# Attention with its join one head behind: statistics, scalings and loads in another order

## The chip, the cores and the metric

The kernel runs on one core of one Trainium2 chip. The metric is the device time of one execution in microseconds; lower is better. The core has a matrix engine (PE), a vector engine (DVE), a scalar engine (ACT), GpSimd (POOL) and SyncE (SP), whose queue issues nearly all DMAs of this kernel. Each engine runs its own instructions in a fixed order and waits on semaphores for the others.

## The reference

A decoder trunk of two layers on 1024 tokens of width 1024, in float32. Layer 0 mixes tokens by dilated attention in three groups (window 128 at dilation 1, 512 at 4, 2048 at 16) with 8 heads of 128; layer 1 by gated linear attention. Each is followed by an MLP of width 4096 with a squared ReLU. The change is in layer 0's attention, so the rest is left out here:

```python
def dilated_group_attention(q, k, v, dil, n_back):
    ...
    s = jnp.where(mask, s, -jnp.inf)
    m = jnp.max(s, axis=-1, keepdims=True)
    p = jnp.exp(s - m)
    l = jnp.sum(p, axis=-1)
    o = jnp.einsum('bzhnqk,bzhnkd->bzhnqd', p, vb) / l[..., None]
    lse = m[..., 0] + jnp.log(l)
    ...

def dilated_attention(h, w_in, w_out):
    B, S, _ = h.shape
    qkv = (h @ w_in).reshape(B, S, N_GROUPS, 3, ATTN_HEADS, HEAD_DIM)
    cos, sin = rope_tables(S, HEAD_DIM)
    outs, lses = [], []
    for g, (window, dil) in enumerate(DILATED_GROUPS):
        q = apply_rope(qkv[:, :, g, 0], cos, sin) * (HEAD_DIM ** -0.5)
        k = apply_rope(qkv[:, :, g, 1], cos, sin)
        v = qkv[:, :, g, 2].astype(jnp.float32)
        o_g, lse_g = dilated_group_attention(q, k, v, dil, window // dil)
        outs.append(o_g)
        lses.append(lse_g)
    alpha = jax.nn.softmax(jnp.stack(lses, axis=0), axis=0)
    o = jnp.sum(alpha[..., None] * jnp.stack(outs, axis=0), axis=0)
    return o.reshape(B, S, ATTN_WIDTH).astype(h.dtype) @ w_out
```

So the three groups' outputs of a head are added with weights that depend on the maximum `m` and the sum `l` of all three groups' rows. The kernel scales the exponentials `p` by these weights (the "scaled probabilities") and then multiplies by the values.

## The kernel before, in words

**Planes and slots.** Layer 0's q and k columns are computed in 24 planes, `p = 3h + g` for head `h` and group `g`. A plane is a product of the normed tokens with 256 columns by a seven-product scheme, each product in two halves of six matmuls: 14 slots, at the end of each of which `advance()` runs what an agenda holds for that slot. `at(slot, fn, rank)` puts a function there; functions of one slot run by rank. This order of calls is the order of the instructions on every engine, so a slot number or a rank in the code moves instructions between neighbours of the same engine, and nothing else does.

**Weights of the next plane.** `load(p + 1)` (L1436) issues four DMAs on SP that bring the raw weights, `stage` splits and combines them on ACT (L791) and DVE (L792, L819, L820, L828, L829).

**Columns and ropes.** Products accumulate in PSUM. `keep` copies a bank to `e` on ACT (L1484), `column` adds a bank and an `e` on DVE (L1444) to `c`, two DMAs (L1445, L1446) write `c` with its halves swapped to `cw`, and some slots later the rope (`turn` in `column`: L1453, L1454 and L1456, or L1461 for groups 1 and 2) makes a half of `qT` or `kT` from both on DVE.

**Scores.** One plane behind, `follow(p - 1)` computes the scores of group `g` (PE L1203, or L1292 for group 2, the "classes"), reduces them on DVE (L1225, L1301), takes the exponential on ACT (L1227, L1303), and `send` writes the statistics `st` (maxima and sums) to DRAM (L1234, L1308).

**The join of a head.** When head `h - 1` has its three groups, `Join(h - 1)` runs across the second plane of head `h`, in the steps that `join_steps` lists by slot:

- `begin` loads all statistics (L1344, L1345, L1348); `factors` makes the weights of the groups on DVE and ACT (L1358 to L1364, ACT at L1360).
- `spread` multiplies the exponentials by the factors: groups 0 and 1 block by block on ACT (L1239), group 2 in one DVE instruction (L1311).
- `load_values` loads `v` of each group (L1178 group 0, L1181 group 1, L1186 group 2).
- `turn_classes` transposes group 2's scaled exponentials on PE (L1318), `copy_classes` copies them to `pt` on ACT (L1388), `values_classes` multiplies by `v` (PE L1326), `keep_classes` copies the result to `oc` (ACT L1394).
- Groups 0 and 1 follow in halves: `turn` (PE L1262), `copy` (ACT L1400), `values` (PE L1271); `join` adds `oc` (DVE L1411).

PE runs all this between the matmuls of the plane (L854). The tables `HEAD` and `LAST` hold the slots of these steps, counted from the slot of `factors`. The last head's join runs in `tail`, among the output projection's matmuls (L196 to L198), with the loads of earlier heads' outputs (`turned.load`, L1798, and `early`, L1842) and of rows of x (`load_x`, L1780) on the same SP queue.

Of the kernel before, what the change touches and what calls it, by code (L numbers as in the profile page):

```python
# [27 lines left out]
NG = 3  # L28
# [13 lines left out]
def hybrid_trunk(ctx, tc, x, norm_mix, norm_mlp, norm_fin, a_in, a_out, g_in, g_up, g_b, g_nw,  # L42
# [219 lines left out]
    class Split:  # L262
# [4 lines left out]
        @staticmethod  # L267
        def at(tiles, k):
            n = 4 // len(tiles)
            return tiles[k // n][:, k % n, :]  # L270
# [1008 lines left out]
            at(c + send, self.send)  # L1279

    class Classes(Attention):
        SOFT = 9, 9, 9, 10
        SEND = 11

        def scores(self, j):
# [132 lines left out]
    class Heads(Up):  # L1418
# [20 lines left out]
        def column(self, p, b, half, bank_, e):  # L1439

            h, g = divmod(p, NG)
            c = t2([P, 512], F32, "c")
            w = t2([P, 512], F32, "cw")
            dve.tensor_tensor(c, bank_, e, op=OP.add)  # L1444
            sp.dma_start(w[0:64, :], c[64:128, :])  # L1445
            sp.dma_start(w[64:128, :], c[0:64, :])  # L1446

            def turn():
                sl = slice(512 * half, 512 * half + 512)
                if (p, b) not in self.dst:  # L1450
                    self.dst[p, b] = k4([P, S], F32, ("qT", "kT")[b])
                dst = self.dst[p, b]
                dve.tensor_tensor(w, w, ctab[:, 1, sl], op=OP.mult)  # L1453
                dve.tensor_tensor(c, c, ctab[:, 0, sl], op=OP.mult)  # L1454
                if g == 0:
                    dve.tensor_tensor(dst[:, sl], c, w, op=OP.add)  # L1456
                else:
                    r = 4 if g == 1 else 16
                    n = 512 // r
                    o = dst.rearrange("p (r m) -> p r m", r=r)[:, :, n * half:n * half + n]  # L1460
                    dve.tensor_tensor(o, c.rearrange("p (m r) -> p r m", r=r),  # L1461
                                       w.rearrange("p (m r) -> p r m", r=r), op=OP.add)
            wait = 3 if p == self.count - 1 and half else 4
            if g == 0 and half:
                wait = (5, 8)[b]
            at(clock[0] + wait, turn, 6)

        def remain(self, fn):
# [7 lines left out]
        def plan(self, p):  # L1476
            c = 14 * p
            st = self.st.setdefault(p, {})
            self.behind = True

            def keep(b, name):
                def fn():
                    e = t2([P, 512], F32, name)
                    act.activation(e, st[b], AF.Copy)  # L1484
                    st[name] = e
                return fn
            at(c + 3, keep("X", "e1"), 0)
            at(c + 5, lambda: self.column(p, 0, 0, st["Y"], st["e1"]), 1)
            at(c + 7, keep("V", "e5"), 0)
            at(c + 9, keep("X", "e2"), 0)  # L1490
            at(c + 11, lambda: self.column(p, 1, 0, st["V"], st["e2"]), 1)
            at(c + 13, keep("X", "e3"), 0)
            at(c + 13, lambda: self.column(p, 1, 1, st["X"], st["e5"]), 1)
            at(c + 15, lambda: self.column(p, 0, 1, st["Z"], st["e3"]), 1)
            if p == 0:
                for s, t in ((4, 1), (6, 3), (5, 5)):
                    at(c + t, lambda s=s: self.stage(p, s), 7)
            at(c + 3, lambda: self.load(p + 1), 5)
            for s, t in ((0, 8), (1, 9), (2, 10), (3, 11), (4, 14), (6, 15), (5, 17)):
                at(c + t, lambda s=s: self.stage(p + 1, s), 1.5 if s in (1, 3, 6) else 7)  # L1500

# [11 lines left out]
        def follow(self, p, c, points=None, soft=None, send=None):  # L1513
            h, g = divmod(p, NG)
            a = groups[h, g] = (Classes if g == 2 else Attention)(g, h, None, None)
            points = points or self.POINTS

            def begin():
                a.qT, a.kT = self.dst.pop((p, 0)), self.dst.pop((p, 1))
            at(c + points[0], begin, 0)  # L1520
            a.plan(c, points, soft or a.SOFT, send or a.SEND)

# [25 lines left out]
        keep_head(h, half, o)  # L1548
        reached.add((0, half))

    HEAD = dict(s2=2, v2=-1, v1=1, sp0=(0, 1, 1, 2), t2=4, o2=5)
    LAST = dict(s2=1, v2=1, v1=4, sp0=(1, 1, 3, 3), t2=5, o2=6)

    def join_steps(load, first, w, gap=1):

        n = lambda k: first + int(gap * k)
        t = 5
        pairs = ((0, 2), (4, 6), (1, 3), (5, 7))
        steps = [(load, 5, "begin"), (n(0), 9, "factors"), (n(w['s2']), 9.1, "spread", 2, None)]
        steps += [(n(w['v2']), 4, "load_values", 2), (n(1), 5, "load_values", 0), (n(w['v1']), 5, "load_values", 1)]  # L1560
        steps += [(n(w['sp0'][i]), 9, "spread", 0, range(2 * i, 2 * i + 2)) for i in range(4)]
        steps += [(n((5, 5, 7, 7)[i]), 9, "spread", 1, pairs[i]) for i in range(4)]
        steps += [(n(w['t2']), 3, "turn_classes"), (n(w['o2']), 0.6, "copy_classes"),
                  (n(w['o2']), 4, "values_classes"), (n(7), 0.5, "keep_classes")]
        order = ((0, 0), (1, 0), (0, 1), (1, 1))
        for i, (g, half) in enumerate(order):
            steps += [(n(t + i), 3, "turn", g, half), (n(t + i + 1), 0.6, "copy", g, half),
                      (n(t + i + 1), 0.65, "values", g, half)]
        return steps + [(n(t + 3), 0.5, "join", 0), (n(t + 5), 0.6, "join", 1)]
# [200 lines left out]
    class Turned:  # L1770
# [6 lines left out]
        def load_x(self, tb):  # L1777
            if tb < NB and tb not in self.loaded:
                self.loaded.add(tb)
                sp.dma_start(self.xs[tb // 2][:, tb % 2, :], self.src_x[128 * tb:128 * tb + 128, :])  # L1780
# [27 lines left out]
    for p in range(heads.count):  # L1808
        h, g = divmod(p, NG)
        if g == 0 and h:  # L1810
            Join(h - 1, joined).plan(14 * p, join_steps(15, 21, HEAD))
        if p == heads.count - 1:
            for k in range(0, KT, 2):
                add_rows(a_out, k)
            c = 14 * p
            at(c + 1, lambda: turned.load(0), 0)
            at(c + 3, lambda: (W.dma(), W.dma()), 0)
            at(c + 4, lambda: (W.dma(), W.dma()), 0)
            for t in (7,8,9,10):
                at(c + t, lambda: W.prep(dve), 7)  # L1820
            at(c + 8, lambda: turned.turn(0), 7)
            at(c + 9, lambda: (turned.load_x(0), turned.load_x(1)))
            at(c + 11, lambda: turned.turn(1), 7)
        heads.run_head(p)
# [7 lines left out]
    def tail():  # L1832

        c = clock[0]
        heads.follow(heads.count - 1, c, (7, 7, 8, 8), (9, 9, 10, 10), 11)
        turned.load(1)
        Join(HEADS - 1, last_joined).plan(c, join_steps(15, 19, LAST, 1.5))
        rows = {}

        def early(half):  # L1840
            t = rows[half] = h8([P, 4, 512], F32, "ol2")
            sp.dma_start(t[:, 0:3, :], oscr[4:7, :, 512 * half:512 * half + 512].rearrange("h p c -> p h c"))  # L1842

        def turn(half, h):
            keep_head(h, half, rows[half][:, h - 4, :])

        def weights():
            W.early = RAW
        at(c + 1, lambda: early(0))
        at(c + 28, weights)  # L1850
        at(c + 20, lambda: early(1))
        for t, half, h in ((10, 0, 4), (12, 0, 5), (14, 0, 6), (33, 1, 4), (35, 1, 5), (37, 1, 6)):
            at(c + t, lambda half=half, h=h: turn(half, h))
        steps.extend([advance] * 60)
# [4 lines left out]
    def out_proj(layer, wbc_row, o, up):  # L1859
# [37 lines left out]
        for tb in range(NB):  # L1897
            if tb in (1, 2) and not layer:
                o.turn(tb + 1)
            load_x(tb + 2)  # L1900
            if tb == (NB - 1 if layer else 3):
                W.limit = 6
                W.early = RAW
            if tb == NB - 1:
                last_block(w)
                continue
            for n in range(2):
                add_block(tb, lambda k: o.parts(tb, k), w, n)
        drain_to((layer, 0))
        W.second = pool  # L1910
        W.limit = 5
# [1 line left out]
        wbc = load_norm_w(wbc_row)  # L1913
        st = Halves(xs, wbc, up, xmid)
        for tb in range(NB):
            if tb == 2:
                drain_to((layer, 1))
                if not layer:
                    steps.clear()
            for n in range(2):  # L1920
                if n:
                    st.middle(tb)
                add_block(tb, lambda k: tuple(t[:, k % 2, 128 * (tb % 4):128 * (tb % 4) + 128]
                                              for t in oT1[tb // 4, k // 2]), w, n)
            st.after(tb)
# [728 lines left out]
```

## Time and profile before

| | before |
|---|---|
| median of 3 runs | 2603.68 us (2602.95 to 2604.55) |
| the profiled execution | 2605.39 us, span 2603.3 us, mean granted clock 0.997 |
| PE, DVE, ACT busy | 2565.1, 1853.8, 1273.1 us |
| layer 0's heads on PE (230 to 860 us) | 607.1 of 630.0 us busy |
| DMA | 519.96 MB, 367511 packets, mean 200 GB/s |

The span is the time between the first and the last instruction of the profiled execution; 2.1 us lie around it. "PE pP L1318 <- DVE pr L1311: 12.3, 7, 3.0" means that PE's instructions of line 1318, which write `pP`, waited for DVE's line 1311 for 12.3 us in all, in 7 places, at most 3.0 us. In a timeline, a bracket behind a row is the idle time of that engine ahead of it and what ended it. On SP, a row is the issue of a DMA, and the landing comes later.

### The profile page before, as it was taken

Reading aid. Unit: us, or ns where it says so; the run is one execution under the profiler, and the core shown is the slowest. Engines: PE = TensorE matmul, PEld = TensorE weight load, DVE = VectorE, ACT = ScalarE, POOL = GpSimd, SP = SyncE. Lnnn points to the kernel's source line nnn. Section 1 sums busy time; section 2 is a strip of 40 time slices with the busy share of each in tenths; the row PEclk is TensorE's granted clock in tenths of the full one; section 3 lists DMA queues with packets and bytes.
Section 4 is the critical chain, followed back from the end, with each engine's and each line's share of the span. In section 5 each row is a group of like instructions: output and inputs, shape, how many; then the busy total and the mean of one; then the engine's idle time right before and its main releaser. Section 6 shows DMA issues by size and latency. Waiting matters only on the chain.

```text
span 2603.3 us, 33979 instructions
## 1 busy us (share of the span) xinstructions
PE 2565.1 (99%) x12391; PEld 2125.5 (82%) x12391; DVE 1853.8 (71%) x2926; ACT 1273.1 (49%) x2243; POOL 17.9 (1%) x26
## 2 busy tenths in 40 slices
PE   9999999999999999999999999999999999999999
PEld 7888888788887788888888888888888888888887
DVE  8766977787778646778768786777666566656567
ACT  7443455545555344566544553564335455553344
POOL 0000000000000000000000000010000000000000
PEclk9999999999999999999999999999999999999999
DMA  5785455443554646699898866777545644396644
GB/s 189 251 288 177 98 111 119 99 109 91 110 118 99 187 155 238 230 322 327 294 341 286 299 202 220 255 250 271 191 159 210 235 161 151 129 349 203 186 151 132
DMA packets 367511, 519.96 MB, mean 200 GB/s; under 512 B 73216, under 2 KB 188688, under 8 KB 367344
## 3 DMA queue, kind: packets, MB, share of 16 engines
q1 hardware_dynamic: 367040, 517.40, 62.0%
q8 instruction: 97, 1.59, 0.3%
q14 instruction: 70, 0.57, 0.1%
q10 hardware_dynamic: 304, 0.40, 0.0%
HBM read 327.20 MB, written 165.35 MB: 189 GB/s over the span
## 4 chain that ended last, share of the span: by engine, by line
PE 86%; DVE 5%; DMA 4%; issue 2%; ACT 1%; SPq 1%; DVEq 0%; ACTq 0%
PE pX L854 15%; PE pB L2006 13%; PE pA L2006 10%; PE pV L854 10%; PE pB L1066 8%; PE pA L1066 6%; PE pZ L854 5%; PE pY L854 5%; DMA cw<-c 3%; PE pd L196 2%; PE pd L198 2%; PE pd L197 2%; PE pO L1271 2%; DVE c L1444 1%; PE pS L1203 1%
## 5 line engine op out<-in xcount | busy, mean ns | idle before, releaser
L2006 PE MATMUL pB<-dl,dh 128*128 128x512 f32 x512 | 199.2, 389 | 0.0
L2006 PE MATMUL pB<-dh 128*128 128x512 f32 x512 | 199.2, 389 | 0.0
L2006 PE MATMUL pB<-dh,dl 128*128 128x512 f32 x512 | 199.2, 389 | 0.0
L205 DVE TENSOR_TENSOR dl<-sin,dh 128x1024 fp32r<-128x1024 f32 x112 | 136.8, 1221 | 63.6 <-ACT dh L202 60.6
L854 PE MATMUL pV<-s4h,wd 128*128 128x512 f32 x480 | 161.3, 398 | 0.0
L202 ACT ACTIVATE dh<-sin 128x1024 fp32r<-128x1024 f32 x112 | 117.8, 1052 | 77.2 <-PE pB L2006 29.8
L2006 PE MATMUL pA<-dh 128*128 128x512 f32 x384 | 149.6, 390 | 0.0
L2006 PE MATMUL pA<-dh,dl 128*128 128x512 f32 x384 | 149.4, 389 | 0.0
L2006 PE MATMUL pA<-dl,dh 128*128 128x512 f32 x384 | 149.4, 389 | 0.0
L859 ACT ACTIVATE e<-pX 128x512 f32<-128x512 f32 x108 | 64.5, 597 | 158.8 <-PE pX L854 158.6
L202 ACT ACTIVATE dh<-kept 128x1024 fp32r<-128x1024 f32 x64 | 67.8, 1060 | 147.1 <-DVE kept L1971 103.2
L2006 PEld LDWEIGHTS pB<-dh 128*128 128x128 f32 x512 | 96.1, 188 | 20.0
L2006 PEld LDWEIGHTS pB<-dl,dh 128*128 128x128 f32 x512 | 96.1, 188 | 20.0
L2006 PEld LDWEIGHTS pB<-dh,dl 128*128 128x128 f32 x512 | 96.1, 188 | 19.9
L854 PEld LDWEIGHTS pV<-s4h,wd 128*128 128x128 f32 x480 | 90.1, 188 | 19.2
L854 PE MATMUL pX<-s3h,wgh 128*128 128x512 f32 x240 | 97.7, 407 | 5.4 <-ACT e L1484 5.4
L854 PE MATMUL pZ<-a22h,wgh 128*128 128x512 f32 x240 | 96.7, 403 | 0.0
L854 PE MATMUL pX<-a11h,wah 128*128 128x512 f32 x240 | 96.4, 402 | 0.0
L854 PE MATMUL pX<-s3h,wgl 128*128 128x512 f32 x240 | 94.5, 394 | 0.0
L854 PE MATMUL pY<-a12h,wah 128*128 128x512 f32 x240 | 94.4, 393 | 0.0
L854 PE MATMUL pX<-s3l,wgh 128*128 128x512 f32 x240 | 94.4, 393 | 0.0
L854 PE MATMUL pX<-a11h,wal 128*128 128x512 f32 x240 | 93.6, 390 | 0.0
(381 smaller groups left out, 7113.9 us busy)
## 6 DMA issues: line engine op xcount, KB each, us to landing
sin<-acts SPq DMA_DIRECT2D x112, 512.0 KB, 4.9
acts<-s SPq DMA_DIRECT2D x64, 512.0 KB, 3.5
raw<-in_mlp_w_down_dram SPq DMA_DIRECT2D x64, 512.0 KB, 5.2
raw<-in_attn_w_in_dram SPq DMA_DIRECT2D x96, 256.0 KB, 5.4
cw<-c SPq DMA_DIRECT2D x192, 128.0 KB, 2.4
raw<-in_mlp_w_up_dram SPq DMA_DIRECT2D x48, 512.0 KB, 6.1
acts<-c SPq DMA_DIRECT2D x64, 256.0 KB, 2.6
kept<-in_mlp_w_down_dram SPq DMA_DIRECT2D x32, 512.0 KB, 7.6
```

Of the source, the lines that this page charges most:

```text
L196: pe.matmul(ps, sh, mh, start=start, stop=False)
L197: pe.matmul(ps, sh, ml, start=False, stop=False)
L198: pe.matmul(ps, sl, mh, start=False, stop=stop)
L202: act.activation(hi, src, AF.Copy)
L205: dve.tensor_tensor(lo, src, hi.bitcast(F32), op=OP.subtract)
L854: pe.matmul(st[b], u[:, k, :], v, start=first and k + n == 0, stop=k == 3 and n == 2, skip_group_check=True)
L859: act.activation(e, self.st[p]["X"], AF.Copy)
L1066: pe.matmul(self.acc[s][t], parts[k][v == 2][:, 128 * t:128 * t + 128], (th, tl)[v == 1][:, k, :], start=fresh and m + k + v == 0, stop=m ...
L1203: pe.matmul(ps[:, i, :128 * n], self.qT[:, 128 * b:128 * b + 128], self.kT[:, k0:k0 + 128 * n], start=True, stop=True)
L1271: pe.matmul(o, self.v[:, k, :], t[:, at_:at_ + n], start=self.g == 0 and i == 0, stop=True, skip_group_check=True)
L1444: dve.tensor_tensor(c, bank_, e, op=OP.add)
L2006: pe.matmul(self.acc[s][t], a[:, k, c], b[:, k, :], start=fresh and m + k + v == 0, stop=m == 7 and k == 1 and v == 2, skip_group_check=True)
```

## The change

Seven things are put in another place; the computation and the number of instructions on PE, DVE and ACT stay.

1. In the plane of group 0 the raw weights of the next plane are loaded at slot 1 and not 3, ahead of the statistics' send.
2. `begin` of a join stands at slot 16 and not 15. Nothing on SP changes place by that.
3. Group 2's scaling (`s2`) stands directly behind the factors and not two slots later. The rope of the second half of group 0's `kT` waits 9 slots (8), that of the first half of group 1's `qT` 6 (4).
4. Group 0's scalings (`sp0`) stand at 2, 3, 6, 6 (0, 1, 1, 2).
5. Group 1's values are loaded at 4 (1), in the heads and in the last one; `v0` names the slot of group 0's values.
6. The third of the four batches of group 2's reductions stands a slot later (`SOFT`).
7. In the last head, `turned.load(1)`, both `early` loads and `load_x(2)` are put off, the copy of the classes has another rank (`o2c`), and the second part of the tail's steps is drained one block later.

`dst.pop` becomes a plain look-up, since a rope now comes after `follow`'s `begin`; it makes no instruction.

```diff
     class Classes(Attention):
-        SOFT = 9, 9, 9, 10
+        SOFT = 9, 9, 10, 10
...
             if g == 0 and half:
-                wait = (5, 8)[b]
+                wait = (5, 9)[b]
+            elif g == 1 and not half and not b:
+                wait = 6
             at(clock[0] + wait, turn, 6)
...
-            at(c + 3, lambda: self.load(p + 1), 5)
+            at(c + (1 if p % NG == 0 and p else 3), lambda: self.load(p + 1), 5)
...
-                a.qT, a.kT = self.dst.pop((p, 0)), self.dst.pop((p, 1))
+                a.qT, a.kT = self.dst[p, 0], self.dst[p, 1]
...
-    HEAD = dict(s2=2, v2=-1, v1=1, sp0=(0, 1, 1, 2), t2=4, o2=5)
-    LAST = dict(s2=1, v2=1, v1=4, sp0=(1, 1, 3, 3), t2=5, o2=6)
+    HEAD = dict(s2=0, v2=-1, v0=2, sp0=(2, 3, 6, 6), t2=4, o2=5, o2c=0.6)
+    LAST = dict(s2=1, v2=1, v0=1, sp0=(1, 1, 3, 3), t2=5, o2=6, o2c=1.2)
...
-        steps += [(n(w['v2']), 4, "load_values", 2), (n(1), 5, "load_values", 0), (n(w['v1']), 5, "load_values", 1)]
+        steps += [(n(w['v2']), 4, "load_values", 2), (n(w['v0']), 5, "load_values", 0), (n(4), 5, "load_values", 1)]
...
-            Join(h - 1, joined).plan(14 * p, join_steps(15, 21, HEAD))
+            Join(h - 1, joined).plan(14 * p, join_steps(16, 21, HEAD))
...
-        turned.load(1)
+        at(c + 1, lambda: turned.load(1), 2)
...
-        at(c + 1, lambda: early(0))
+        at(c + 3, lambda: early(0))
         at(c + 28, weights)
-        at(c + 20, lambda: early(1))
+        at(c + 28, lambda: early(1))
...
-            load_x(tb + 2)
+            if tb or layer:
+                load_x(tb + 2)
...
+            if not tb and not layer:
+                load_x(2)
...
-            if tb == 2:
+            if tb == (2 if layer else 3):
                 drain_to((layer, 1))
```

**DVE, the second head's join, before**: from the last instruction of the factors (L1364) to group 2's scaling (L1311). L1225 are the reductions of group 0's scores, L1453 to L1461 a rope, `wal` and `t` steps of the next weights.

```order
L1364 TENSOR_TENSOR stat<-stat,mz 128x72
L1225 ISA pr,st<-pS,masks 128x128
L1225 ISA st 128x1
L1225 ISA pr,st<-pS,masks 128x256
L1225 ISA st 128x1
L1453 TENSOR_TENSOR cw<-cw,tab 128x512
L1454 TENSOR_TENSOR c<-c,tab 128x512
L1461 TENSOR_TENSOR qT<-c,cw 128x4x128
L792 TENSOR_TENSOR wal<-raw,wah 128x512
L1311 TENSOR_TENSOR pr<-pr,stat 128x512
```

The same place after, from the second half of group 0's `qT`:

```order
L1456 TENSOR_TENSOR qT<-c,cw 128x512
L1358 TENSOR_REDUCE mz<-stat 128x24
L1359 TENSOR_TENSOR stat<-mz,stat 128x72
L1361 TENSOR_TENSOR stat<-stat 128x72
L1362 TENSOR_REDUCE mz<-stat 128x24
L1363 RECIPROCAL mz<-mz 128x24
L1364 TENSOR_TENSOR stat<-stat,mz 128x72
L1311 TENSOR_TENSOR pr<-pr,stat 128x512
L1453 TENSOR_TENSOR cw<-cw,tab 128x512
L1454 TENSOR_TENSOR c<-c,tab 128x512
L1456 TENSOR_TENSOR kT<-c,cw 128x512
```

The scaling moved from behind the rope of group 1's `qT` (L1461) to directly behind the factors, and the factors from behind the rope of `kT` to ahead of it. The rope of group 1's `qT` now stands behind the next four reductions.

**ACT, the same join, before**: from the exponential of the factors (L1360) to the first scores' exponentials (L1227). L1239 are group 0's scalings, `e` is the bank copy that the next product waits for.

```order
L1360 ACTIVATE stat<-stat 128x72
L1239 ACTIVATE pr<-pr,stat 128x128
L1239 ACTIVATE pr<-pr,stat 128x256
L791 ACTIVATE wah<-raw 128x512
L1239 ACTIVATE pr<-pr,stat 128x256 x4
L1484 ACTIVATE e_3747<-pX 128x512
L791 ACTIVATE wah<-raw 128x512
L1227 ACTIVATE pr,st<-pr,st 128x128
```

After:

```order
L1360 ACTIVATE stat<-stat 128x72
L791 ACTIVATE wah<-raw 128x512
L1486 ACTIVATE e_3737<-pX 128x512
L791 ACTIVATE wah<-raw 128x512
L1227 ACTIVATE pr,st<-pr,st 128x128
L1227 ACTIVATE pr,st<-pr,st 128x256
L1239 ACTIVATE pr<-pr,stat 128x128
L1239 ACTIVATE pr<-pr,stat 128x256 x3
```

Six scalings stood ahead of `e`, none does now. Four of them come behind the first exponentials. Later on ACT in the same join, before, from group 0's first `pt` copies to the next ones (`oc` is group 2's result):

```order
L1400 ACTIVATE pt<-pP 128x512
L1400 ACTIVATE pt<-pP 128x384
L1227 ACTIVATE pr,st<-pr,st 128x256 x2
L1394 ACTIVATE oc<-pO 128x4x2x64 x2
L1400 ACTIVATE pt<-pP 128x512
```

After:

```order
L1400 ACTIVATE pt<-pP 128x512
L1400 ACTIVATE pt<-pP 128x384
L1227 ACTIVATE pr,st<-pr,st 128x256 x2
L1239 ACTIVATE pr<-pr,stat 128x256 x4
L1394 ACTIVATE oc<-pO 128x4x2x64 x2
L1400 ACTIVATE pt<-pP 128x512
```

The other four scalings of group 0 stand ahead of `oc` and of group 1's `pt`.

**SP, the same join, before**: the value loads.

```order
L1436 DMA raw<-in_attn_w_in_dram 128x4x128 x4
L1445 DMA cw<-c 64x512
L1446 DMA cw<-c 64x512
L1186 DMA v<-vscr 64x8x128 x2
L1178 DMA v<-vscr 128x8x128
L1181 DMA v<-vscr 128x4x128 x2
```

After:

```order
L1436 DMA raw<-in_attn_w_in_dram 128x4x128 x4
L1445 DMA cw<-c 64x512
L1446 DMA cw<-c 64x512
L1186 DMA v<-vscr 64x8x128 x2
L1178 DMA v<-vscr 128x8x128
L1445 DMA cw<-c 64x512
L1446 DMA cw<-c 64x512
L1181 DMA v<-vscr 128x4x128 x2
```

Group 1's two loads moved behind the next pair of `cw`; the raw loads and the pair behind them kept their places.

**SP, the last head, before**: `ol` and `xs` are loads for the output projection, the last two `cw` belong to the rope of the last `qT` half.

```order
L1798 DMA ol<-oscr 128x4x512
L1780 DMA xs<-in_x_dram 128x1024
L1445 DMA cw<-c 64x512
L1446 DMA cw<-c 64x512
L1842 DMA ol_7757<-oscr 128x3x512
L1234 DMA stats_80<-st 512x2x2
```

After:

```order
L1445 DMA cw<-c 64x512
L1446 DMA cw<-c 64x512
L1800 DMA ol<-oscr 128x4x512
L1234 DMA stats_80<-st 512x2x2
L1844 DMA ol_7778<-oscr 128x3x512
L1782 DMA xs<-in_x_dram 128x1024 x3
```

The `cw` pair now goes ahead of `ol` and `xs`, and the statistics ahead of the second load of outputs.

More of the change, by code (lines that the diff above doesn't have):

```diff
@@ L1559, in join_steps @@
         steps = [(load, 5, "begin"), (n(0), 9, "factors"), (n(w['s2']), 9.1, "spread", 2, None)]
-        steps += [(n(w['v2']), 4, "load_values", 2), (n(1), 5, "load_values", 0), (n(w['v1']), 5, "load_values", 1)]
+        steps += [(n(w['v2']), 4, "load_values", 2), (n(w['v0']), 5, "load_values", 0), (n(4), 5, "load_values", 1)]
         steps += [(n(w['sp0'][i]), 9, "spread", 0, range(2 * i, 2 * i + 2)) for i in range(4)]
         steps += [(n((5, 5, 7, 7)[i]), 9, "spread", 1, pairs[i]) for i in range(4)]
-        steps += [(n(w['t2']), 3, "turn_classes"), (n(w['o2']), 0.6, "copy_classes"),
+        steps += [(n(w['t2']), 3, "turn_classes"), (n(w['o2']), w['o2c'], "copy_classes"),
                   (n(w['o2']), 4, "values_classes"), (n(7), 0.5, "keep_classes")]
```

## The prediction

> **What bounds the kernel now.** I read three views in this order: the page's busy times, all waits of PE, and then the timeline around one wait of each kind.
>
> ```profile
> PE 2565.1 (99%) x12391; PEld 2125.5 (82%) x12391; DVE 1853.8 (71%) x2926; ACT 1273.1 (49%) x2243; POOL 17.9 (1%) x26
> ...
> PE pP L1318 <- DVE pr L1311: 12.3, 7, 3.0
> PE pX L854 <- ACT e L1484: 5.4, 7, 1.8
> PE pS L1292 <- DVE qT L1461: 4.2, 2, 3.8
> PE pO L1326 <- ACT pt L1388: 4.0, 5, 0.8
> ```
>
> PE is busy 2565.1 of 2603.3 us, so 38.2 us of idle time are all that a reordering can win; PE's own order is the same in both kernels. Of them, 12.3 + 5.4 + 4.0 = 21.7 us lie in the seven joins of heads 0 to 6 (total, times, longest in each row). One wait of 3.8 us lies in the last head. The second head's join shows all three kinds, first on PE (start, duration, operation, and in brackets the idle time ahead):
>
> ```profile
> 421.69 0.50 PE L854 MATMUL pX<-s3h,wgh 128*128 128x512 f32 x1 [0.26 <-ACT e L1484]
> 422.03 0.40 PE L854 MATMUL pX<-s3l,wgh 128*128 128x512 f32 x1
> ...
> 424.86 0.66 PE L1318 MATMUL pP<-ident,pr 128*128 128x128 f32 x4 [1.50 <-DVE pr L1311]
> ...
> 429.33 0.88 PE L1326 MATMUL pO<-pt,v 64*128 64x64 f32 x11 [0.80 <-ACT pt L1388]
> ...
> 436.14 1.05 PE L1271 MATMUL pO<-pt,v 128*128 128x128 f32 x8
> ```
>
> A wait also costs a restart: the first matmul behind it takes 0.50 us, the second 0.40, so 0.10. Without its waits, PE would come to the transposes L1318 at 424.86 - 1.50 - 0.26 - 0.10 = 423.0, to L1326 at 429.33 - 2.56 - 0.2 = 426.6, and to the values of group 1 (the last row) at 436.14 - 2.56 - 0.3 = 433.3. These are the due times. DVE in the same place:
>
> ```profile
> 414.34 0.69 DVE L1453 TENSOR_TENSOR cw<-cw,tab 128x512 f32<-128x512 f32 x1
> ...
> 416.27 0.22 DVE L1358 TENSOR_REDUCE mz<-stat 128x24 f32<-128x72 f32 x1
> ...
> 418.11 0.28 DVE L1225 CUSTOM_DVE_ANT_0 pr<-pS,masks 128x128 f32<-128x128 f32 x1
> ...
> 421.18 0.69 DVE L1453 TENSOR_TENSOR cw<-cw,tab 128x512 f32<-128x512 f32 x1 [2.43 <-DMA cw<-c]
> ...
> 424.13 0.67 DVE L1311 TENSOR_TENSOR pr<-pr,stat 128x512 f32<-128x512 f32 x1
> ...
> 427.25 0.42 DVE L1225 CUSTOM_DVE_ANT_0 pr<-pS,masks 128x256 f32<-128x256 f32 x1
> ```
>
> The factors are ready at 418.1, but the scaling L1311 that needs them starts at 424.13: ahead of it stands the rope of group 1's first q half, which waits 2.43 us for its swapped copy `cw`. SP's queue says why that copy is late:
>
> ```profile
> 412.31 2.21 SPq L1436 DMA_DIRECT2D raw<-in_attn_w_in_dram  x4
> 414.62 0.49 SPq L1445 DMA_DIRECT2D cw<-c  x1
> ...
> 417.94 4.37 SPq L1181 DMA_DIRECT2D v<-vscr  x2
> ...
> DMA to landing us min/median/max: 6.0/6.1/6.1
> ...
> cw<-c SPq DMA_DIRECT2D x192, 128.0 KB, 2.4
> ...
> DMA to landing us min/median/max: 6.1/7.3/8.3
> ```
>
> The fourth row is of `cw` here (6.1 us to land, behind four raw loads), the fifth its median over the kernel (2.4), the sixth that of the value loads `v` here. ACT, last:
>
> ```profile
> 419.46 1.69 ACT L1239 ACTIVATE pr<-pr,stat 128x256 f32<-128x256 f32 x4
> 421.06 0.58 ACT L1484 ACTIVATE e<-pX 128x512 f32<-128x512 f32 x1
> ...
> 427.70 0.51 ACT L1227 ACTIVATE pr<-pr,st 128x256 f32<-128x256 f32 x1 [0.48 <-DVE st L1225]
> ...
> 428.70 0.57 ACT L1388 ACTIVATE pt<-pP 128x512 f32<-128x512 f32 x1
> 429.18 1.26 ACT L1239 ACTIVATE pr<-pr,stat 128x128 f32<-128x128 f32 x4
> ...
> 430.82 0.96 ACT L1400 ACTIVATE pt<-pP 128x512 f32<-128x512 f32 x2
> ...
> 433.08 1.92 ACT L1394 ACTIVATE oc<-pO 128x512 f32<-128x512 f32 x2
> 434.96 0.60 ACT L1400 ACTIVATE pt<-pP 128x512 f32<-128x512 f32 x1
> ```
>
> Group 0's spreads (L1239) stand ahead of the copy `e` that the next matmuls read; the copy `pt` (L1388) stands behind exponentials that wait for DVE's late reductions at 427.25. The last cost shows in the granted clock (columns: window, PE busy, clock, DMA share, GB/s):
>
> ```profile
> 507.00:510.00 3.00, 2.96 (x10) 0.57 0.06 16
> 589.00:592.00 3.00, 2.89 (x10) 0.55 0.25 64
> 829.00:832.00 3.00, 2.92 (x16) 1.00 0.16 41
> 888.50:894.50 6.00, 6.00 (x28) 0.62 0.13 46
> ```
>
> PE's wait for L1311 in the join of the third head (502 to 508 us), the fourth (585 to 590) and the seventh (825 to 835):
>
> ```profile
> PE pP L1318 <- DVE pr L1311: 3.0, 1, 3.0
> ...
> PE pP L1318 <- DVE pr L1311: 2.1, 1, 2.1
> ...
> PE pP L1318 <- DVE pr L1311: 2.2, 1, 2.2
> ```
>
> Behind the third and fourth head's waits, and behind the last head's, the clock is halved for a while. A window at clock x holds 2(1 - x) of its length at half speed, of which half is lost: 3 x 0.43 = 1.3, 3 x 0.45 = 1.35, and 6 x 0.38 = 2.3 us. Behind the seventh head's waits (829) nothing is lost.
>
> **The change, part by part.**
>
> *Scaling directly behind the factors (HEAD s2, ropes later), DVE.* The factors now start where the second half of group 0's k rope started, 414.34, and take 418.11 - 416.27 = 1.84, so to 416.2; L1311 ends 416.9, 6.1 us before PE's due time of 423.0. All seven waits on L1311 should go: 12.3. The k rope (1.93, as 414.34 to 416.27) ends at 418.8 rather than 416.3; the scores that read this half come after the pair that PE runs ahead of the due time, so it is hidden. The q rope that waits for `cw` moves behind the second score reductions and its product is read one plane later; what now stands ahead of the reductions is two score reductions and five weight and column steps (0.6 to 0.7 each) from 418.8, so they start near 422.5 instead of 427.25.
>
> *Copy `e` ahead of the spreads, ACT.* The four spreads of 1.69 straight ahead of it leave, and two more before them. It ends by about 421.64 - 1.69 = 419.9 against a due time of 421.69 - 0.26 = 421.4: the 5.4 go.
>
> *Copy `pt` of the third group.* Reductions from 422.5, exponentials 428.70 - 427.70 = 1.0 behind them, then 0.57: it ends near 425.0, due 426.6. The 4.0 go in an undisturbed join. In the third, fourth and seventh head (the longest waits for L1311) the raw loads land later, and DVE's weight steps now stand ahead of the reductions: up to 1 us stays there.
>
> *Four spreads moved ahead of `oc` (sp0 entries 6, 6), ACT.* From 425.0: four small spreads, `e` and two copies (429.18 to 431.78: 2.6) to 427.6; exponentials to 428.6; the four spreads, 1.69, to 430.3; `oc`, 1.92, to 432.2; `pt` of group 1, 0.60, to 432.8. Due 433.3. This is the tightest place: half a microsecond of margin, none where something is 1 us late. I take 0.3 in four heads, and 1.33 in the three late ones for this and the last step together: 5.2 us in all, between 0 and 13 (1.8 in all seven).
>
> *SP's queue.* Raw loads of the plane after group 0 go ahead of the statistics' send. Four issues are 2.21 us, so the send leaves up to 2.2 us later, and its reader, the statistics' load, stands a plane behind: 0, or up to 0.3 per head if that queue is full. The first 'raws, then `cw`' order at 412 is the same, so `cw` still lands late; now nobody who matters stands behind it. Group 1's two value loads move behind the next `cw` pair, whose column ends near 422.1: issued from about 423.3, the second from about 423.9, landing 6.1 to 8.3 later, so 430.0 to 432.2 against 433.3: hidden, with 1.1 us left at the worst.
>
> *Last head.* One row each of SP, DVE and PE:
>
> ```profile
> 876.87 0.47 SPq L1445 DMA_DIRECT2D cw<-c  x1
> ...
> 884.66 0.69 DVE L1453 TENSOR_TENSOR cw<-cw,tab 128x512 f32<-128x512 f32 x1 [2.44 <-DMA cw<-c]
> ...
> 887.09 1.98 PE L1292 MATMUL pS<-kT,qT 128*64 128x64 f32 x32 [3.83 <-DVE qT L1461]
> ```
>
> DVE was free at 884.66 - 2.44 = 882.2 and waited for a `cw` pair issued at 876.87, 7.8 us before. The pair now goes ahead of an `ol` and an `xs` load; at 2.4 us it is there long before 882.2, and DVE's 2.44 go; the wait on PE falls from 3.83 to 1.4. With so short a wait I let the 2.3 of slow clock go too: 4.7 (2.4 if it stays, 6.1 if the whole wait goes). The other loads that are put off there (`ol2`, an `xs` row, the later drain) I cost at 0, up to 2 us lost if one is late, since their readers stand 10 us and more behind.
>
> *Sum.* Heads: 21.7, restarts 19 x 0.10 = 1.9, slow clock 1.3 + 1.35 = 2.65, together 26.25; less 5.2 that stay is 21.05. With 4.7 it makes 25.75. The profiled execution took 2605.39 (span 2603.3 and 2.1 around it), so it becomes 2579.6; the median of the runs is 1.71 lower, 2603.68 - 25.75 = 2577.9, forecast as 2578.
>
> The slow clock is where a rule and the rows part. The Trainium skill (TensorE: Matmul & The Clock Gate, § HAM oscillation — how this bites in real kernels) puts the loss at idle gaps over about 3.4 us. The rows show it behind gaps of 3.0 and 2.1 us in the third and fourth head, and no loss behind the seventh head's 2.2; only the last head's 3.83 is as long as the rule wants. If by that rule the two heads' 2.65 come from something else and stay, the sum would be 23.1 and the time 2580.6.
>
> **The rivals.**
>
> *Half of it stays at the next copy.* The four spreads hold up group 1's `pt` in each join. For it speaks the margin of 0.5 us in a chain of eight steps; against it that the margin is there in the row-by-row sum of an undisturbed join. 1.8 in each of seven heads and 4.0 for the late ones is 16.6 instead of 5.2: 2589.3. With the last head's gain gone as well, 2594.
>
> *Slower: group 1's values come late.* Their loads now stand on SP behind a `cw` pair, which waits for DVE's column and for a buffer; PE waits at L1271. It costs more than all that is won (25.75 + 5.2, 4.4 a head, or 3.1 and a slow clock of 1.3) from a landing at 433.3 + 3.1 = 436.4, 13 us behind the issue. No `v` here took over 8.3. At 14 us in each join the time is about 2611.
>
> *No change: the statistics hold the factors.* L1311 needs the factors; if the statistics landed at 420 or later (factors 1.84 and L1311 0.67 before 423.0), DVE would stand still there, and everything behind it. They are in by 416.27 in the trace, since DVE did not wait. About 2 us later in every join would only eat slack; at 3.5 later the old waits are back: 2603.
>
> **How the numbers follow.** Forecast case (2571 to 2583) 0.62; half of it 0.26 (2584 to 2596); no change 0.05; slower 0.07. Lower end: nothing stays (5.2 more) and the last head gains 6.1: 2571. Upper end: the half case with the last head's gain gone, 2594. Outside stay the two last cases and the edges, under 2 in 10. A change within 0.2% (5.2 us) can't be told from none: faster 0.88, same 0.05, slower 0.07.
>
> **What would show it.** Right: L1318's row of 12.3 and that of `e` nearly gone from PE's waits, L1388 under 2, L1292 near 1.4, L1271 behind L1400 between 2 and 6, PE idle near 15 us, and the clock at 1.00 behind every join. Wrong: L1271 over 10 (first rival), L1271 waiting for a DMA `v` (second), DVE waiting for a DMA `stat` ahead of L1358 (third); or the halved clock still there behind waits of under 1 us.

## The result and the profile after

The changed kernel takes 2573.96 us (median of 4 runs, 2573.47 to 2574.16) against 2603.9 us: the ratio is 0.9885 with a 95% interval of 0.9868 to 0.9902, so it is about 30 us faster. The profiled execution took 2573.8 us, 31.6 less than that of before. The page's first part, and PE's waits (total, times, longest):

```profile
PE 2556.6 (99%) x12391; PEld 2122.4 (83%) x12391; DVE 1852.4 (72%) x2926; ACT 1271.2 (49%) x2243; POOL 17.9 (1%) x26
```

```profile
PE pO L1271 <- ACT pt L1400: 2.7, 3, 1.1
...
PE pS L1292 <- DVE qT L1461: 1.3, 1, 1.3
PE pP L1318 <- ACT pr L1239: 0.8, 1, 0.8
```

PE's idle time fell from 38.2 to 2571.7 - 2556.6 = 15.1 us. The 12.3 us on L1311, the 5.4 on `e` and the 4.0 of L1326 are gone without a rest. Two waits of 0.85 and 0.73 us at L1271 are left in the heads (the third of that line, 1.1, was in the last head before as well), and one of 0.8 at L1318 is new in the last head, behind a scaling of group 0 on ACT.

Because PE runs the same instructions in the same order, the start of the same matmul in two traces tells how much was won up to it. In the second head's join, PE after:

```profile
419.45 0.60 PE L1318 MATMUL pP<-ident,pr 128*128 128x128 f32 x4
...
423.00 2.00 PE L1326 MATMUL pO<-pt,v 64*128 64x64 f32 x32
...
429.53 0.40 PE L854 MATMUL pZ<-a22h,wgl 128*128 128x512 f32 x1
429.99 1.16 PE L1271 MATMUL pO<-pt,v 128*128 128x128 f32 x8
```

No row has a bracket. The first two and the last started at 424.86, 429.33 and 436.14 before. DVE and ACT there:

```profile
413.24 0.69 DVE L1311 TENSOR_TENSOR pr<-pr,stat 128x512 f32<-128x512 f32 x1
...
417.86 0.69 DVE L820 TENSOR_TENSOR t<-raw,t 128x512 f32<-128x512 f32 x1 [0.23 <-DMA raw<-in_attn_w_in_dram]
...
419.67 0.42 DVE L1225 CUSTOM_DVE_ANT_0 pr<-pS,masks 128x256 f32<-128x256 f32 x1
...
420.35 0.69 DVE L1453 TENSOR_TENSOR cw<-cw,tab 128x512 f32<-128x512 f32 x1
```

```profile
421.14 0.57 ACT L1388 ACTIVATE pt<-pP 128x512 f32<-128x512 f32 x1
...
425.96 1.69 ACT L1239 ACTIVATE pr<-pr,stat 128x256 f32<-128x256 f32 x4
427.56 1.96 ACT L1394 ACTIVATE oc<-pO 128x512 f32<-128x512 f32 x2
429.32 0.62 ACT L1400 ACTIVATE pt<-pP 128x512 f32<-128x512 f32 x1
```

L1311 is done 5.5 us before PE comes. The rope that waited 2.43 us for `cw` now starts at 420.35 without a wait, and the second reductions (419.67) no longer stand behind it. On ACT the four scalings, `oc` and `pt` follow each other without a hole up to 429.94, and PE's L1271 starts at 429.99: the chain that the prediction called the tightest ends just when PE starts. PE even stood for about 0.2 us there, too little for a bracket: from the matmul ahead of it (429.53) to L1271 are 0.46 us, and 0.23 in the kernel late4 below, where `pt` is early.

The same comparison of start times for every kernel (us won against before; "heads" is from the matmul at 335 to that at 850 us of before, "last head" from there to 940; one execution each, and two executions of the changed kernel differ by 0.1 in the heads and 1.3 in the last head):

| kernel | median of its runs | heads | last head |
|---|---|---|---|
| after | 2573.96 | 26.2 | 4.5 |
| after, second time | 2574.19 | 26.2 | 3.2 |
| rope | 2580.78 | 23.6 | -0.7 |
| scale | 2608.35 | -15.4 | 2.2 |
| copy | 2609.66 | -8.0 | 0.5 |
| ropecopy | 2576.88 | 26.1 | 3.1 |
| rope4 | 2612.73 | -14.2 | 5.6 |
| old_sp | 2577.68 | 22.5 | 3.7 |
| no_raw | 2577.18 | 22.2 | 3.5 |
| old_v1 | 2574.85 | 25.8 | 4.0 |
| old_tail | 2577.16 | 27.1 | 0.7 |
| best | 2571.50 | 29.3 | 4.0 |
| late4 | 2571.48 | 29.5 | 4.3 |

Of the 31.6 us between the profiled executions of before and after, 26.2 + 4.5 are in these two columns; the other 0.9 lies ahead of the matmul at 335, where the executions scatter by 1.5. A profiled execution is not always a typical one: those of scale (2618.77), copy (2613.31), rope (2581.95) and no_raw (2579.00) were the slowest of their kernel, that of ropecopy (2575.30) the fastest of its four, of which one took 2584.21.

The changed kernel ran a second time in the last group of experiments:

> The changed kernel again, beside the others of this group on the same chip: 2574 us, within 1.5 of the first time, L1271 0.7 to 0.9 in two heads, the clock at full speed behind every join.

It took 2574.19 us there, with waits of 0.68 and 0.91 at L1271 in the same two heads. The 1.3 us that its last head won less are three waits: 1.3 instead of 0.8 at L1318, 0.6 instead of 0.2 at L1203, and 0.5 at L1271 for a load of values.

The kernel before took 2603.6, 2604.1 and 2603.4 us beside the three groups of four experiments. Its single runs spread there from 2599.8 to 2609.8, so differences under 2 us are read from the traces alone.

### The profile page after: what moved, and what is told of

It is laid out like the page before. It is cut to its first block, busy times and chain, and to the rows that moved or that the text cites. A ratio compares the mean times of both kernels' runs of the same rounds, so it can differ in the third digit from the quotient of the medians.

```text
span 2571.7 us, 34000 instructions
## 1 busy us (share of the span) xinstructions
PE 2556.6 (99%) x12391; PEld 2122.4 (83%) x12391; DVE 1852.4 (72%) x2926; ACT 1271.2 (49%) x2243; POOL 17.9 (1%) x26
## 4 chain that ended last, share of the span: by engine, by line
PE 92%; DMA 2%; DVE 2%; ACT 2%; SPq 1%; issue 1%; DVEq 0%; ACTq 0%
PE pX L854 18%; PE pB L2011 14%; PE pV L854 12%; PE pA L2011 10%; PE pB L1066 8%; PE pA L1066 6%; PE pY L854 6%; PE pZ L854 6%; PE pd L196 2%; PE pd L198 2%; PE pd L197 2%; PE pO L1271 2%; PE pS L1203 1%; PE pP L1262 1%; DMA raw<-in_attn_w_in_dram 1%
## 5 line engine op out<-in xcount | busy, mean ns | idle before, releaser
L854 PE MATMUL pZ<-a22h,wgl 128*128 128x512 f32 x240 | 93.7, 390 | 0.0
```

Source lines behind the costliest of these rows:

```text
L854: pe.matmul(st[b], u[:, k, :], v, start=first and k + n == 0, stop=k == 3 and n == 2, skip_group_check=True)
```

## The experiments

**One edit at a time, on the kernel before.** The theory: PE waits at three places, but DVE has one chain, whose slowest link is the rope that waits for `cw`. Rivals: three independent waits, or an order of the scalings that matters by itself.

*rope*: only the rope of group 1's first q half, two slots later.

```diff
             if g == 0 and half:
                 wait = (5, 8)[b]
+            elif g == 1 and not half and not b:
+                wait = 6
```

> Before with one edit: the rope of group 1's first q half waits 6 slots instead of 4 (and the plain look-up that this needs). Theory of the one chain: L1318 waits only because L1311 stands behind a rope that waits for its swapped copy, and L1326 only because the second reductions stand behind the same rope. Then this edit alone takes L1318's 12.3 us, L1326's 4.0, 1.2 of restarts and 2.65 of slow clock; the 5.4 on e stay: 2603.9 - 20.2 = 2584 us (2582 to 2588), L1318 under 1, L1326 under 1, e 5 to 6. Rival, the scaling must stand directly behind the factors: L1318 still waits, behind the weight step that needs raw loads; gain under 6, 2598 or more. Rival, the copy of e is what is late and the rest follows from it: no change.

It took 2580.78 us against 2603.61 (ratio 0.9908, 0.9893 to 0.9923): 22.8 us faster by this one number, where 20.2 were expected; 1.5 of the difference is that the waits on `e` shrank from 5.4 to 3.9. PE's waits, and DVE in the second head:

```profile
PE pX L854 <- ACT e L1486: 3.9, 7, 1.5
```

```profile
417.68 0.68 DVE L1311 TENSOR_TENSOR pr<-pr,stat 128x512 f32<-128x512 f32 x1
...
420.88 0.41 DVE L1225 CUSTOM_DVE_ANT_0 pr<-pS,masks 128x256 f32<-128x256 f32 x1
...
421.56 0.69 DVE L1453 TENSOR_TENSOR cw<-cw,tab 128x512 f32<-128x512 f32 x1
```

L1311 and the second reductions stand ahead of the rope, and nothing waits for `cw` any more. The scaling need not stand directly behind the factors.

*scale*: L1311 directly behind the factors, and the rope stays.

```diff
-    HEAD = dict(s2=2, v2=-1, v1=1, sp0=(0, 1, 1, 2), t2=4, o2=5)
+    HEAD = dict(s2=0, v2=-1, v1=1, sp0=(0, 1, 1, 2), t2=4, o2=5)
```

> Before with one edit: group 2's scaling L1311 directly behind the factors (s2=0); the rope that waits for its swapped copy stays ahead of the second reductions. Theory of the one chain: L1318's 12.3 go, but PE meets the same chain again at L1326, whose pt stands behind the reductions; only L1311's 0.6 us leave the chain: 0.6 in five heads, 1.4 in the third and fourth, 5.8 in all: 2598 us (2595 to 2602), L1318 under 0.5, L1326 from 4.0 to about 13.5, e 5.4 as before. Rival, the waits are independent: L1318's 12.3 with 0.7 of restarts and 2.65 of slow clock go, 2588, L1326 stays at 4.

```profile
PE pO L1326 <- ACT pt L1388: 18.5, 7, 4.3
PE pX L854 <- ACT e L1484: 4.0, 7, 1.4
```

L1318 is gone from the list, and L1326 grew from 4.0 to 18.5: the wait moved, as the theory said, and further. The time went the other way, 2608.35 us (ratio 1.0016, 1.0002 to 1.0029), where 2598 was expected: a miss of 10 us. Why, PE shows in the second head, with the clock (columns as in the prediction) there, and behind the fourth head:

```profile
433.00 2.85 PE L1326 MATMUL pO<-pt,v 64*128 64x64 f32 x32 [1.90 <-ACT pt L1388]
435.78 0.79 PE L854 MATMUL pZ<-a22h,wgh 128*128 128x512 f32 x1
436.38 0.63 PE L854 MATMUL pZ<-a22l,wgh 128*128 128x512 f32 x1
```

```profile
433.00:436.00 3.00, 3.00 (x33) 0.68 0.16 36
436.00:439.00 3.00, 3.00 (x8) 0.50 0.39 87
...
601.70:604.70 3.00, 3.00 (x37) 1.00 0.11 24
```

A wait of 1.90 us, 0.4 longer than the one it replaced (1.50, behind which nothing was lost), halved the clock: the 32 small matmuls took 2.85 instead of 2.00 us and the next six 0.42 each from start to start instead of 0.23. In the fourth head a wait of 2.00 us at the same place cost no clock at all. How often the clock falls differs from execution to execution: the mean granted clock of the ten is 0.991 to 0.995, and the profiled one, with 0.991, is the slowest, so its -15.4 in the table is more than the 4.7 us that the median lost.

*copy*: ACT's scalings from ahead of `e` to where the change has them.

```diff
-    HEAD = dict(s2=2, v2=-1, v1=1, sp0=(0, 1, 1, 2), t2=4, o2=5)
+    HEAD = dict(s2=2, v2=-1, v1=1, sp0=(2, 3, 6, 6), t2=4, o2=5)
```

> Before with one edit: group 0's scalings on ACT at slots 2, 3, 6, 6 and not 0, 1, 1, 2, so that none stands ahead of e. Theory of the one chain: the 5.4 on e go, and PE comes earlier to L1318, which waits for DVE as before: L1318 from 12.3 to about 17.7, only 0.7 of restarts are won: 2603 us (2601 to 2606, the upper part if the longer waits halve the clock in more heads). Rival, independent waits: 5.4 and 0.7 won, 2597.8, L1318 still near 12.3.

```profile
PE pP L1318 <- DVE pr L1311: 21.9, 7, 5.4
```

```profile
424.54 0.69 DVE L1453 TENSOR_TENSOR cw<-cw,tab 128x512 f32<-128x512 f32 x1 [3.10 <-DMA cw<-c]
```

```profile
428.20:431.20 3.00, 3.00 (x17) 1.00 0.04 10
...
836.30:839.30 3.00, 3.00 (x10) 0.50 0.16 40
```

The waits on `e` are gone and nothing is won: they are in L1318 now, with 4.2 more than the 17.7 expected. In the second head `cw` landed later too (DVE waited 3.10 for it here and 2.43 before); why, and whether that makes all of the 4.2, was not tested. With the clock halved behind five of the seven waits, at 836 among them, the kernel is slower than before, 2609.66 us (ratio 1.002, 1.001 to 1.003). At 428 a wait of 2.70 us did not halve it.

*ropecopy*: both edits.

> Before with the two edits together: the rope of group 1's first q half at 6 slots, and the scalings on ACT at 2, 3, 6, 6. Everything else as before: scaling L1311 two slots behind the factors, raw loads behind the statistics, value loads early, the last head untouched. Theory of the one chain: what the whole change won in the heads, 26.5 us by the start times of the same matmuls, comes back: 2577.4 us (2576 to 2580), and the sum of the two single edits (about 20 and 1) is smaller than the pair. Rival, the earlier factors, the raw loads or the value loads carry a part: 2582 or more, with waits left at L1318 or at L1271 for a DMA.

2576.88 us (0.99, 0.9884 to 0.9916), and, in the fastest of its four executions, 26.1 us won in the heads, as with the whole change. One edit wins 22.8, the other loses 6.1, the two together win 26.7: the first opens DVE's chain, and only then is the second worth its 3.9.

**Undoing one part of the whole change.**

*rope4*: the two lines taken out of the changed kernel.

```diff
-            elif g == 1 and not half and not b:
-                wait = 6
```

> After with one edit undone: the rope of group 1's first q half waits 4 slots again, so that it and its late swapped copy stand ahead of the second score reductions. All else of the change stays. Theory of the one chain: this single edit carries the heads. L1326 waits for pt behind those reductions as in the kernel with the scaling alone (18.5 us there) plus what e took there (4.0): about 22 in seven heads, and a halved clock behind most of them, 2 to 3 us each; the last head keeps its gain of 4.5. 2603 us (2598 to 2609), slower than after by 25 to 34. Rival, the earlier factors, scaling and scalings carry it together: at most 10 slower than after, 2584.

```profile
PE pO L1326 <- ACT pt L1388: 19.9, 7, 3.4
```

```profile
424.37 0.69 DVE L1453 TENSOR_TENSOR cw<-cw,tab 128x512 f32<-128x512 f32 x1 [2.50 <-DMA cw<-c]
```

```profile
432.00:438.00 6.00, 6.00 (x38) 0.51 0.59 146
...
761.50:767.50 6.00, 6.00 (x39) 0.55 0.55 144
```

2612.73 us (ratio 1.0032 against before, 1.0022 to 1.0041), above the 2598 to 2609 expected: without one number the whole change is a loss. Of the 40.4 us by which its heads fall behind after's (26.2 + 14.2), 18.3 are waits (19.9, where after has 1.6); the other 22 fit the clock, which is halved behind each of the seven, for 51 us in all.

*old_sp*, *no_raw* and *old_v1*: the queue edits in the heads taken back, both, and each alone.

```diff
-            at(c + (1 if p % NG == 0 and p else 3), lambda: self.load(p + 1), 5)
+            at(c + 3, lambda: self.load(p + 1), 5)
...
-        ... (n(4), 5, "load_values", 1)]
+        ... (n(1), 5, "load_values", 1)]
```

The second line is shortened; with it, `v0` is 1 again in old_sp and old_v1, and `begin` at slot 15 in old_sp.

> After with its queue edits undone in the heads: raw loads behind the statistics' send again, group 1's values ahead of the cw pair, begin at slot 15. Theory: none of this is on the path; the swapped copy that is late has nobody behind it that PE waits for. Same as after within 1.5 us, with waits only at L1271 behind ACT's pt, up to 3 us in all in the heads. Rival, the queue order is what frees the loads: over 5 us slower, with waits for a DMA or at L1271, L1326 in each head.

This was a miss: old_sp lost 3.6 us in the heads (22.54 against 26.15), with waits of 1.0 to 1.2 us at L1326 and L1271 in the third head and at L1271 in the fourth and seventh, and 0.3 at L1326 in the seventh. Which edit it was:

> After with one queue edit undone: in the plane of group 0, the raw loads of the next plane stand behind the statistics' send again. Theory, from the kernel with both queue edits undone (4.4 us slower by the matmuls' start times, with waits at L1326 and L1271 in the third, fourth and seventh head): behind that send, which takes over 5 us to land, the raw loads land up to 3.8 us later, which makes the third head's whole chain late. Then this edit carries it: 3 to 5 us slower than after, the third head's waits of about 1 at L1326 and L1271 back. Rival, the value loads ahead of the cw pair carry it: same as after within 0.7.

> After with the other queue edit undone: group 1's values are loaded ahead of the next cw pair again. Theory of the raw loads: same as after within 0.7 us by the matmuls' start times, no more waits than there. Rival, the value loads carry the 4.4 us: 3 to 5 us slower than after with waits at L1271 in three heads.

no_raw has 22.2 in the heads and 2577.18 us, old_v1 25.8 and 2574.85: the raw loads carry most of it. By the medians no_raw is 3.0 us behind the changed kernel beside it; of the 4.0 by start times, about 1.5 are the clock, halved behind its wait of 1.03 us at L1326 in the third head (windows and columns as in the prediction):

```profile
499.75:503.16 3.41, 2.38 (x36) 1.00 0.80 203
503.16:506.57 3.41, 3.41 (x9) 0.50 0.47 112
```

SP's queue in the third head of no_raw with the time to land of these four loads, then the same of after:

```profile
461.63 0.65 SPq L1234 DMA_DIRECT2D stats<-st  x1
462.32 2.38 SPq L1436 DMA_DIRECT2D raw<-in_attn_w_in_dram  x4
...
DMA to landing us min/median/max: 6.7/6.9/9.1
```

```profile
461.06 2.29 SPq L1436 DMA_DIRECT2D raw<-in_attn_w_in_dram  x4
463.45 0.65 SPq L1234 DMA_DIRECT2D stats<-st  x1
...
DMA to landing us min/median/max: 3.9/4.3/4.7
```

Behind the send the loads take 6.9 us to land, ahead of it 4.3 (medians of the four; over the six planes of group 0 from 385 us on they are 6.5 to 7.3 in no_raw and 3.6 to 4.9 in after). They carry the weights of the plane that runs beside the join, and some 34 us later the third head's join is late on DVE, where a weight step waits for the next raw loads (the steps between the two were not followed one by one):

```profile
496.93 0.69 DVE L820 TENSOR_TENSOR t<-raw,t 128x512 f32<-128x512 f32 x1 [0.97 <-DMA raw<-in_attn_w_in_dram]
```

That is so beside the other edits of the whole change only. In ropecopy the loads go behind the send too and take 6.8 to 6.9 us, and its heads win as much as after's: it loses 1.3 us to after in the third head and 0.4 in the fourth, and wins 0.9 in the seventh, where it has no wait at L1271, and smaller amounts in the rest. Which of the other edits makes the seventh head late was not tried.

*old_tail*: the last head's edits taken back, with `SOFT`.

```diff
-        at(c + 1, lambda: turned.load(1), 2)
+        turned.load(1)
...
-        at(c + 3, lambda: early(0))
+        at(c + 1, lambda: early(0))
...
-            if tb == (2 if layer else 3):
+            if tb == 2:
```

> After with the last head's edits undone: ol, ol2 and xs loads where they were, the old rank of the classes' copy, the old SOFT. Theory: the cw pair is again behind ol and xs, L1292 waits 3.1 to 3.8 instead of 1.3; 2 us lost, and 2.3 more if the clock is halved behind it (it was not in one of the kernels with two edits, at 3.27); the 0.8 at L1318 may go: 1.5 to 4 us slower than after. Rival, the last head's gain comes with the heads' and not from its own edits: same as after within 0.5, L1292 near 1.3.

```profile
PE pS L1292 <- DVE qT L1461: 3.4, 1, 3.4
```

```profile
847.38 0.59 SPq L1800 DMA_DIRECT2D ol<-oscr  x1
848.31 0.34 SPq L1782 DMA_DIRECT2D xs<-in_x_dram  x1
848.76 0.47 SPq L1445 DMA_DIRECT2D cw<-c  x1
```

```profile
858.50:861.50 3.00, 3.00 (x35) 0.50 0.73 191
```

2577.16 us, and 0.7 us won in the last head instead of 4.5: the `cw` pair is again behind `ol` and `xs`, and the clock is halved behind the wait. The whole block of edits was undone at once; which of them pays besides the `cw` pair was not tried. One of them costs: in the heads, where of all that old_tail takes back only `SOFT` stands, it won 27.1 and not 26.2, and the two waits at L1271 are 0.51 and 0.42 instead of 0.85 and 0.73. So the later third batch of reductions loses about 0.9 us in the heads (in one execution).

**A version that beats both.**

*late4*: the last four scalings of group 0 go behind `oc` and group 1's `pt`, still ahead of the transposes that read them.

```diff
-    HEAD = dict(s2=0, v2=-1, v0=2, sp0=(2, 3, 6, 6), t2=4, o2=5, o2c=0.6)
+    HEAD = dict(s2=0, v2=-1, v0=2, sp0=(2, 3, 7, 7), r0=(9, 9, 0.9, 0.9), t2=4, o2=5, o2c=0.6)
...
-        steps += [(n(w['sp0'][i]), 9, "spread", 0, range(2 * i, 2 * i + 2)) for i in range(4)]
+        steps += [(n(w['sp0'][i]), w.get('r0', (9, 9, 9, 9))[i], "spread", 0, range(2 * i, 2 * i + 2)) for i in range(4)]
```

*best* is late4 with another edit, `turned.turn(1)` at `c + 10` instead of `c + 11`.

> After with two more edits: the four scalings at slot 6 go to slot 7 behind oc and group 1's pt (rank 0.9, still ahead of the transposes that read them), and the split of the second pair of earlier heads' outputs for the last plane goes from slot 11 to 10, ahead of exponentials that wait for DVE. Theory: L1271's waits in the heads (0.85 and 0.73, 1.6 with a small one) go, and the 0.77 and 0.53 on oTh and oTl; 3.3 us faster than after by the start times of the same matmuls. Rival, pt waits for the transposes and not for the scalings: L1271 stays at 0.7 to 0.9 where it was; or the split delays DVE's next column and the wait moves to L1203.

> After with only the four scalings moved behind oc and group 1's pt. In the kernel that also moved the split, the heads won 2.0 us and the split's 1.4 were lost again at L1292 with a halved clock. Theory: the heads' 2.0 alone stay, L1292 at 1.3 as in after, no halved clock: 2 us faster than after. Rival, the last head gives it back however PE comes to it: same as after within 0.5, L1292 over 2.

late4 took 2571.48 us beside 2574.19 of the changed kernel on the same chip (0.9877, 0.9862 to 0.9891, against before): no wait is left in the heads, 29.5 us won there. That is 3.3 more than after: 1.1 and 1.2 in the fourth and seventh head, where after's two waits stood, the rest in steps of 0.3 or less. The single runs of the two overlap (2569.97 to 2573.10, 2572.45 to 2574.78), so the start times are the firmer evidence. best is no faster (2571.50): it has removed the waits on the split, and the time is back at L1292, which it pushed from 1.3 to 2.5, with a halved clock behind it (854.95 to 858.36):

```profile
PE pS L1292 <- DVE qT L1461: 2.7, 2, 2.5
```

## Why the prediction was right, point by point

Forecast was 2578 us, 25.75 won; measured were 29.9 (2603.9 to 2573.96), and 31.6 between the two profiled executions. In the heads 21.05 were forecast and 26.2 measured: 3.6 of the difference are waits that did not stay, about 0.4 the clock, and about 1 us is not assigned.

- *L1311 directly behind the factors, 12.3 us; `pt`, 4.0; slow clock 2.65.* Right in amount: all of it went. (The slow clock was read too small. Its two stretches at half speed last 3.41 us each, 507.4 to 510.8 and 589.3 to 592.7, and the windows of 3 us leave out a part of each; at 0.42 instead of 0.23 us from matmul to matmul they cost about 1.5 each and not 1.3 and 1.35.) The prediction put the 12.3 under the scaling's new place. The runs show another cause: the scaling alone loses (scale), the rope alone wins (rope), and without the rope's edit the rest loses (rope4). The prediction had the rope in the same paragraph and counted it for the reductions only.
- *`e`, 5.4 us.* Right within the pair; alone it is worth nothing (copy), because DVE's chain ends later than `e`.
- *What stays in the heads, 5.2 us.* Mis-sized: 1.6 us stayed, in the fourth and the seventh head. The mechanism was right, since the place is L1271 behind `pt` with the four scalings ahead of it, and removing them from there removed the waits (late4). Two smaller holds of about 0.2 at L1271, in the second and third head, are under what the list of waits shows.
- *SP's queue, 0.* This step failed. It priced the send's delay and not what the raw loads win by going first: 2.6 us in landing, and 4.0 us in the heads (26.2 against 22.2, about 1.5 of it clock). With it undone the heads keep about the waits that were forecast for them: 4.9 us in old_sp against the 5.2 forecast, in the third, fourth and seventh head. So the two errors are one: the late heads were taken as given, and in the whole change the raw loads ahead of the send make them punctual.
- *`SOFT`.* It has no term in the prediction; old_tail shows about 0.9 us lost by it in the heads.
- *The value loads.* Right: old_v1 differs by 0.4 us in the heads.
- *Last head, 4.7.* Measured 4.5 and, the second time, 3.2. The sum was met in part by luck: the slow clock was worth about 2.7 and not 2.3 (half speed until 893.1, PE busy from 887.1), and the new wait of 0.8 at L1318 was not forecast. L1292 fell to 1.3 (1.4 forecast), and the slow clock behind it went:

```profile
858.50:864.50 6.00, 6.00 (x28) 1.00 0.83 300
```

- *The rivals.* Half of it staying at the next copy fell, since 1.6 us stayed and not 16.6, but the margin of 0.5 us was gone: in the second head `pt` held PE for about 0.2. The slower case needed value loads 13 us late; the statistics held nothing up.
- *The rule on the clock.* The prediction weighed the Trainium skill (TensorE: Matmul & The Clock Gate, § HAM oscillation — how this bites in real kernels), which puts the loss at gaps over about 3.4 us, and kept the two heads' slow clock among the gains against it. That was right: the clock is full behind every join of after, and the runs halve it behind gaps of 1.03 us (no_raw, 501 us), 1.69 (scale, 761 us) and 1.90.

## What to carry to other kernels

On an in-order engine, find the instruction that waits for a transfer and move that one; moving something else shifts the wait to another consumer, as scale and copy did. Waits that look separate in a list of totals can be links of one chain, so an edit that is worth 4 us behind another can be worth nothing, or cost, alone. When loads that feed the next stage meet a small scattered store on the same queue, price the load's landing on both sides of it and not only the store's.

## What the runs showed of the hardware

The length of a gap does not decide whether the matrix engine's clock is halved behind it. In these traces gaps of 1.03, 1.69, 1.84, 1.90 and 2.58 us halved it, and 2.00, 2.70 and 3.27 did not, the last as in this row of ropecopy behind its 3.27 at L1292:

```profile
859.40:862.40 3.00, 3.00 (x41) 1.00 0.87 202
```

The gaps of 3.38 us and more did in every case.

The clock records of the traces show most of what decides. In the heads and the last head every stretch at half speed begins a whole multiple of 3.413 us behind the trace's first clock record (which lies 4.3 to 7.4 us behind the start of the span) and lasts one, two or three such steps. Three steps around the third head's wait in before:

```profile
504.00:507.41 3.41, 0.46 (x4) 1.00 0.89 204
507.41:510.82 3.41, 3.41 (x11) 0.50 0.06 16
510.82:514.23 3.41, 3.41 (x44) 1.00 0.32 70
```

With all 14 traces cut into these steps, from 300 to 960 us, half speed follows every step in which PE idled for 1.9 us or more: 23 of the 27 stretches. The other four follow a step with less idle time (1.84, 1.69, 1.03 and 1.00 us), and in all four the wait is at L1326, with its 64x64 matmuls behind it in the same step. Other steps with up to 1.84 us idle were followed by full speed. So a gap that straddles two steps can pass: 2.70 and 3.27 us leave at most 1.84 and 1.68 in one. This is read from the traces and was not tested by a run of its own, and why less idle time is enough at L1326 stays open. It fits the running window that the Trainium skill (TensorE: Matmul & The Clock Gate, § What's actually happening) describes as free-running.

Each stretch costs a little under half of the time that PE is busy in it: about 1.5 us for one step and 3 to 4 for two or three. That is what made scale and rope4 slower than before, though PE waits 22.5 and 19.9 us in their heads against 21.7.

A statistics send of 8 KB (1024 pieces of 8 bytes) on the same queue put 2.6 us on the landing of the 256 KB loads behind it in the third head (6.9 us against 4.3).
